# Regrouping the neighbourhood-attention stage of a two-layer diffusion backbone: pairs of heads as one step, other PSUM banks, another order of the filling work

## The chip, the cores and the metric

The kernel runs on one NeuronCore of a Trainium2 chip. Its inputs and outputs lie in HBM, everything is one launch. The metric is device time in microseconds (us), the median of several executions. The engines are named as in the profile: PE (TensorE, matrix multiplications and transposes), PEld (PE's weight loads), DVE (VectorE), ACT (ScalarE), POOL (GpSimd) and SP (SyncE, which here only issues DMAs).

## The reference

A backbone of two layers over 256 latent tokens and 256 context tokens of width 1024. Each layer is a half-step SwiGLU, a mixer, and a second half-step SwiGLU, each followed by a LayerNorm with residual. The mixer of layer 0, which this case is about, is neighbourhood attention with 16 heads of width 64: each latent query reads a 2-D window of the latent keys, with a bias for the relative position, and all context keys in the same softmax.

```python
qkv = (hx @ w_qkv).reshape(B, S, 3, N_HEADS, HEAD_DIM)
q = apply_axial_rope(qkv[:, :, 0], rope)
k = apply_axial_rope(qkv[:, :, 1], rope)
...
s_win = jnp.where(mask, s_win + bias.astype(jnp.float32)[None], -jnp.inf)
s_ctx = jnp.einsum('bjqhd,bchd->bhjqc', q_r, k_c).astype(jnp.float32) * scale
p = jax.nn.softmax(jnp.concatenate([s_win, s_ctx], axis=-1), axis=-1).astype(v.dtype)
return (jnp.einsum('bhjqk,bjkhd->bjqhd', p[..., :nk], v_blk)
        + jnp.einsum('bhjqc,bchd->bjqhd', p[..., nk:], v_c))
...
y_lat = jnp.moveaxis(o, 0, 1).reshape(B, S, D) @ w_out
```

The values are float32. The kernel keeps that accuracy by splitting each operand into a high and a low part: a product is three matmuls, high by high, high by low, low by high.

## The kernel before, in words

**Order.** PE's instructions run in the order in which the program writes them. The other engines' instructions are put in order by a scheduler at build time: by priority, which is the place in the program, moved forward by `tc.high_priority(offset=...)`, and by when it thinks that their inputs are there. At run time each engine works through its list in order.

**Units.** A unit is one step of a generator: six matmuls 128x512 (`mmu`, lines 152 to 159), for two chunks of 128 rows of the contraction. `wunit` (L162 to L182) loads the weights for units and splits them, ACT making the high part (L178), DVE the low part (L181). `tick` (L136) counts units. A `Late` (L113) is work that is written into the program so many ticks after it was made, or when somebody calls `get()`.

**PSUM.** There are eight banks in three groups: three "mm", three "at", two "tp". Panels and attention outputs use "mm" (`mmb`, L98), the scores S and the odd row tiles of the output projections use "at", transposes use "tp" (`tpb`).

**The attention stage** (L734 to L933). `q_half` projects and rotates q for eight heads (8 units), `kv_quarter` k and v for four heads (16 units). Each leaves a `Late`, which transposes the result (kT: L771 to L776, qT: L787 to L795) and splits it; `q_half` has a delay of two ticks, `kv_quarter` of one. For a pair of heads and one of two query tiles, `scores` (L804) makes S for both heads in two "at" banks with six matmuls; then per head DVE adds the bias (L818) and takes the maximum (L820), ACT takes the exponential (L822) and scales (L824). `probs_T` (L830) transposes one head's probabilities (L836) and splits them. `values` (L841) multiplies one head's with v into a "mm" bank, and adds the high and the low half of the product (L854, L855); after the second head of a pair the sum is split into oT (L861).

The loop (L902 to L930) runs over half steps, one head of one query tile each. In every second one it writes `scores` for a pair, in each one `probs_T` of the half step two before, and `values` one half step after a head's second `probs_T`. Between them `fill_some` writes units of the fill: first `filler` (k/v quarters 1 and 2, q half 1, k/v quarter 3: 56 units), with a rate of 2.4, 2.9 and 1.9 units per half step, and from half step 24 `last_filler`, which is the output projection (`sub_end`, `out_gemm` with `order_late`, 16 units, of which nine are given out in the loop at a rate of 1.0, and seven come after it).

**The output projection's order** (`order_late`, L421). A unit is (row tile t, column half n, contraction chunk u), with u from 0 to 3; chunk 3 needs the last four heads. Nine units of the three banks (0,0), (0,1), (1,0) with u up to 2 come first, then their u = 3, then all four units of bank (1,1). When row tile 0 is complete its LayerNorm runs, and five ticks later its transposes (hT, L340), on which the next stage begins.

Of the kernel before, what the change touches and what calls it, by code (L numbers as in the profile page):

```python
# [16 lines left out]
P = 128  # L17
# [18 lines left out]
LEAD = 5  # L36
TAIL = 3
XAT = 1
A_LAG = 2
A_PRE = 2  # L40
NX_AT = 2
R0 = 2.4
R1 = 2.9
R2 = 1.9
R3 = 1.0
LN_LAG = (5, 5)
LT_LAG = (5, 5)
F0_LAG = (5, 5, 6, 7)
G_LAG = 4
ROPE_EARLY = 70  # L50
S_EARLY = 40
V_LAG = 1
AHEAD = 3
P_EARLY = 70
V_EARLY = 70
W_HI = 2
# [8 lines left out]
def backbone_kernel(  # L65
# [22 lines left out]
    def nm(s):  # L88
        uid[0] += 1
        return f"{s}_{uid[0]}"  # L90

    def act(dt=F32, s="a"):
        return ap.tile([P, 512], dt, tag="act", name=nm(s))
# [4 lines left out]
    def mmb(s="mm", t=0):  # L98
        return bank("at" if t % 2 else "mm", s)

    def tpb(s="tp"):
        return bank("tp", s)

    def split(src, hi, lo):
        nc.scalar.activation(hi, src, AF.Copy)  # L105
        nc.vector.tensor_tensor(out=lo, in0=src, in1=hi.bitcast(F32), op=ALU.subtract)  # L106
# [311 lines left out]

        return order_skew(nu)[:-TAIL] + [(1, 1, u, c, c + 256) for c in (0, 256) for u in range(nu - TAIL, nu)]

    def order_late(nu):  # L421

        e = nu - 1
        banks = ((0, 0), (0, 1), (1, 0))
        o = [(t, n, u) for t, n in banks for u in range(e - 1)]
        o += [(t, n, u) for u in (e - 1, e) for t, n in banks]
        return o + [(1, 1, u) for u in range(nu)]

    def out_gemm(w, lhs, nk, order, evac, s, wrow0=0):

# [206 lines left out]
    def sub_end(w, lhs, nk, l, i, gm, wgt, nxt, s, order):  # L637


        gate = mod_rows(l, gm, "gate")  # L640
        lnr = None if nxt else ln_rows(l, i)
        GB = fold_cols(nxt[0], 0, nxt[1], (l, i)) if nxt else None
        st, hTs = {}, [None, None]

        def evac(t, n, bank, *c):
            if n == 0:
                st[t] = stat_tile(2 if nxt or t == 0 else 3)
            part = nxt is None and t == n == 1
            cs = slice(*(c or (0, 512)))
            residual(bank, xt[t][n][:, cs], gate[n][:, cs], wgt, None if c else ALPHA,  # L650
                     None if part and not c else st[t][:, n + (c[0] // 256 if c else 0)])
            if n == 1 and (not part or c and c[1] == 512):
                mv, rs = finish_stats(st[t])
                if nxt:
                    hTs[t] = modulated(xt[t], mv, rs, GB, (LN_LAG if nk > KC else LT_LAG)[t])
                else:
                    for h in range(2):
                        nc.vector.scalar_tensor_tensor(out=xt[t][h], in0=xt[t][h], scalar=mv[:, 0:1], in1=lnr[0][h],
                                                       op0=ALU.subtract, op1=ALU.mult)
                    for h in range(2):  # L660
                        nc.vector.scalar_tensor_tensor(out=xt[t][h], in0=xt[t][h], scalar=rs, in1=lnr[1][h],
                                                       op0=ALU.mult, op1=ALU.add)
                        sync.dma_start(out[0, t * P:(t + 1) * P, h * 512:(h + 1) * 512], xt[t][h])

        return out_gemm(w, lhs, nk, order, evac, s), hTs, (lambda: new_x(l, i))
# [86 lines left out]
    def kv_quarter(g, res):  # L752
        krs, v = [], []

        def each(t, bk):
            if t < 2:
                krs.append(roped(bk[:, 0:256], t, 1, 4))
            else:
                r1 = rtile(256)
                nc.scalar.activation(r1, bk[:, 0:256], AF.Copy)  # L760
                krs.append(r1)
            v.append(act(F32R, "v"))
            z = v[t].rearrange("p (h s d) -> p h s d", h=4, s=2)
            split(bk[:, 256:512].rearrange("p (h d) -> p h d", h=4), z[:, :, 0], z[:, :, 1])

        yield from tile_panel(D + g * 256, 2 * D + g * 256, [hTs[t] for t in range(4)], "wkv", each)

        def rest():
            kT = []
            for j in range(2):  # L770
                ps = tpb("kT")  # L771
                for t in range(4):
                    nc.tensor.transpose(ps[:, t * P:(t + 1) * P], krs[t][:, j * P:(j + 1) * P], ident)
                hi, lo = act(F32R, "kTh"), act(F32R, "kTl")
                split(ps, hi, lo)
                kT.append((hi, lo))  # L776
            return kT

        res.append((Late(1, rest), v))

    def q_half(g, res):
        qrs = []
        yield from tile_panel(g * 512, g * 512 + 256, [hTs[0], hTs[1]], "wq", lambda t, bk: qrs.append(roped(bk, t, 0, 8)))

        def rest():
            qT = []
            for j in range(2):  # L787
                ps = tpb("qT")
                for i in range(2):
                    for t in range(2):  # L790
                        nc.tensor.transpose(ps[:, i * 256 + t * P:i * 256 + (t + 1) * P],
                                            qrs[t][:, (2 * j + i) * P:(2 * j + i + 1) * P], ident)
                hi, lo = act(F32R, "qTh"), act(F32R, "qTl")
                split(ps, hi, lo)
                qT.append((hi, lo))  # L795
            return qT

        res.append(Late(2, rest))
# [37 lines left out]
            nc.tensor.transpose(pt[:, k * P:(k + 1) * P], pr[:, k * P:(k + 1) * P], ident)  # L836
        split(pt.rearrange("p (k q) -> p k q", k=4), pth[:, :, qt * P:(qt + 1) * P], ptl[:, :, qt * P:(qt + 1) * P])

    osum = {}

    def values(h):  # L841

        pth, ptl = PT.pop(h)
        ps = mmb("o")[:, 0:256]
        s = slice(h % 4 * P, (h % 4 + 1) * P)
        v = KV[h // 4][1]
        for k in range(4):
            nc.tensor.matmul(ps, v[k][:, s], pth[:, k], start=k == 0, stop=False)
            nc.tensor.matmul(ps, v[k][:, s], ptl[:, k], start=False, stop=k == 3)
        if h % 2 == 0:  # L850
            osum[0] = sp.tile([P, 512], F32, tag="tmp", bufs=3, name=nm("osum"))[:, 0:256]
        p0 = h % 2 * 64
        t = osum[0][p0:p0 + 64]
        nc.scalar.activation(t, ps[64:128], AF.Copy)  # L854
        nc.vector.tensor_tensor(out=t, in0=ps[0:64], in1=t, op=ALU.add)  # L855
        if h % 2:
            if len(oT) <= h // 4:
                oT.append([hp.tile([P, 512], F32R, tag="oT", bufs=6, name=nm("oT")) if len(oT) < 3 else act(F32R, "oT")
                           for _ in range(2)])
            cs = slice((h // 2 % 2) * 256, (h // 2 % 2) * 256 + 256)  # L860
            split(osum[0], *(z[:, cs] for z in oT[h // 4]))  # L861

    phase.__exit__(None, None, None)
    ext[0] = 0
# [12 lines left out]
    def last_filler():  # L877
        with tc.issue_after(bias_dma[-1].ins):
            for t in range(2):
                for h in range(2):  # L880
                    xt[t][h] = act(F32, "x")
                    sync.dma_start(xt[t][h], xscr[t * P:(t + 1) * P, h * 512:(h + 1) * 512])
            gen, nh, lt = sub_end(na_w_out[0], lhs_T(oT), KC, 0, 1, 5, 1.0, (0, 6), "wo", order_late(KU))
        box.extend([nh, lt])
        yield from gen

    box = []
    fill = filler()
    rate = [R0] * 8 + [R1] * 8 + [R2] * 8 + [R3] * 12
    credit = 0.0  # L890
    steps = [(h + i, qt) for h in range(0, NH, 2) for qt in range(2) for i in range(2)]
    prs = {}
    LAG = A_LAG
    fin = None

    def fill_some(n):
# [2 lines left out]
                break  # L899

    fill_some(A_PRE)
    for i in range(len(steps) + LAG + V_LAG):  # L902
        if i == NX_AT:
            new_x(0, 0, s2t)
            for t in range(2):
                for h in range(2):
                    sync.dma_start(xscr[t * P:(t + 1) * P, h * 512:(h + 1) * 512], xt[t][h])
        while i + AHEAD < len(steps) and len(KV) <= steps[i + AHEAD][0] // 4:
            fill_some(1)
        if i < len(steps) and i % 2 == 0:  # L910
            with tc.high_priority(offset=S_EARLY):
                prs[i], prs[i + 1] = scores(*steps[i])
            if i % 2 == 0 and i + 2 < len(steps):
                bias_pair(*steps[i + 2])
        credit += rate[min(i, len(rate) - 1)]
        n = int(credit)
        credit -= n
        if i >= 24 and fin is None:
            run(fill)
            fin = last_filler()  # L920
            fill = islice(fin, 9)
        fill_some((n + 1) // 2)
        if 0 <= i - LAG < len(steps):
            with tc.high_priority(offset=P_EARLY):
                probs_T(*steps[i - LAG], prs.pop(i - LAG))
        fill_some(n // 2)
        j = i - LAG - V_LAG
        if j >= 0 and steps[j][1] == 1:
            with tc.high_priority(offset=V_EARLY):
                values(steps[j][0])  # L930
    run(fill)
    run(fin)
    phase.__exit__(None, None, None)  # L933
# [129 lines left out]
```

## Time and profile before

| | |
|---|---|
| median of 3 runs | 1284.12 us (1282.69 to 1287.56) |
| the profiled execution, its own time | 1289.17 us |
| its span in the trace | 1287.4 us |
| PE busy | 1257.7 us, 98% |
| DVE busy | 955.1 us, 74% |
| ACT busy | 591.2 us, 46% |
| mean granted clock of PE | 0.996 |

The profiled execution is one, and somewhat longer than the median; 1.8 us of its time lie outside of the span. The attention loop lies between about 440 and 589 us of the span, the projection after it ends at about 602 us. In the profile's lists, "idle" is the time in which an engine's instruction waited, and the name behind the arrow is what released it. Matmuls are pipelined, so that the durations of neighbouring ones overlap: the distance between two starts tells more than a duration.

### The profile page before, as it was taken

The numbers are of one execution on the slowest core, as the hardware profiler recorded it, in microseconds if no ns is written. First come the engines' busy times: TensorE is split into PE (matmuls) and PEld (weight loads), VectorE is DVE, ScalarE is ACT, GpSimd is POOL, SyncE is SP. The second block draws the span as 40 slices with busy tenths as digits, with TensorE's granted clock in tenths as the row PEclk, the third lists the DMA queues.
The fourth block names the chain that finished last, engine by engine and source line by source line (L and its number), as shares of the span: only waits on it lengthen the run. The fifth ranks groups of instructions, "written<-read, shape, count | busy, mean of one in ns | idle before, by whom it ended". The sixth has DMA issues, their size and how long they took to land.

```text
span 1287.4 us, 17193 instructions
## 1 busy us (share of the span) xinstructions
PE 1257.7 (98%) x5890; PEld 1007.0 (78%) x5890; DVE 955.1 (74%) x1683; ACT 591.2 (46%) x1148; POOL 42.0 (3%) x71
## 2 busy tenths in 40 slices
PE   7999999999999999988999999999999999999997
PEld 4787778788778877766887787887787877788886
DVE  3699877485658777788998787757778788855545
ACT  2432132413236456686555435654435645655431
POOL 0000000000001111110000000000000000000000
PEclk9999999999999999999999999999999999999999
DMA  9977569484622744464999887666887764666641
GB/s 284 299 231 243 181 193 297 131 297 146 198 78 76 215 91 92 90 147 149 305 331 328 295 294 262 215 215 225 289 287 241 215 211 147 210 217 185 231 155 51
DMA packets 202712, 268.59 MB, mean 209 GB/s; under 512 B 30026, under 2 KB 149298, under 8 KB 202624
## 3 DMA queue, kind: packets, MB, share of 16 engines
q1 hardware_dynamic: 202624, 267.49, 65.9%
q8 instruction: 46, 0.75, 0.2%
q14 instruction: 42, 0.34, 0.1%
HBM read 265.27 MB, written 2.17 MB: 208 GB/s over the span
## 4 chain that ended last, share of the span: by engine, by line
PE 78%; DVE 8%; DMA 8%; ACT 3%; issue 2%; SPq 1%; POOL 0%; DVEq 0%; ACTq 0%
PE w L156 13%; PE w L157 13%; PE w L159 13%; PE f L541 6%; PE f L542 6%; PE f L543 6%; DMA ar<-in_ada_w_dram 5%; DMA w1r<-in_ffn_w_in_dram 2%; PE wkv L156 2%; PE wkv L157 2%; PE wkv L159 2%; PE wc L156 2%; PE wc L157 2%; PE wc L159 2%; DVE w1l L181 2%
## 5 line engine op out<-in xcount | busy, mean ns | idle before, releaser
L178 ACT ACTIVATE w1h<-w1r 128x512 fp32r<-128x512 f32 x352 | 203.3, 626 | 185.0 <-PE w L159 75.4
L181 DVE TENSOR_TENSOR w1l<-w1r,w1h 128x512 fp32r<-128x512 f32 x352 | 227.6, 684 | 66.5 <-ACT w1h L178 64.3
L156 PE MATMUL w<-w1h,hTh 128*128 128x512 f32 x528 | 211.6, 401 | 3.8 <-ACT hTh L105 3.7
L247 DVE SCALAR_TENSOR_TENSOR acc<-ar,cst,acc 128x512 f32<-128x512 f32 x266 | 187.2, 745 | 34.8 <-DMA ar<-in_ada_w_dram 34.8
L157 PE MATMUL w<-w1l,hTh 128*128 128x512 f32 x528 | 207.7, 393 | 0.0
L156 PE MATMUL w<-w2h,gh 128*128 128x512 f32 (+1 forms) x446 | 175.4, 394 | 0.0
L157 PE MATMUL w<-w2l,gh 128*128 128x512 f32 (+1 forms) x446 | 173.7, 390 | 0.3 <-DVE w2l L181 0.3
L178 ACT ACTIVATE w2h<-w2r 128x512 fp32r<-128x512 f32 x176 | 101.5, 624 | 140.9 <-PE w L159 131.6
L159 PE MATMUL w<-w1h,hTl 128*128 128x512 f32 x528 | 163.9, 392 | 0.6 <-DVE hTl L106 0.6
L181 DVE TENSOR_TENSOR w2l<-w2r,w2h 128x512 fp32r<-128x512 f32 x176 | 114.0, 686 | 43.5 <-ACT w2h L178 42.3
L541 PE MATMUL f<-h0h,w1h 128*128 128x512 f32 x352 | 139.8, 397 | 0.4 <-ACT w1h L178 0.4
L542 PE MATMUL f<-h0h,w1l 128*128 128x512 f32 x352 | 138.4, 393 | 0.0
L543 PE MATMUL f<-h0l,w1h 128*128 128x512 f32 x352 | 138.3, 393 | 0.0
L159 PE MATMUL w<-w2h,gl 128*128 128x512 f32 (+1 forms) x446 | 136.3, 387 | 0.0
L156 PEld LDWEIGHTS w<-w1h,hTh 128*128 128x128 f32 x528 | 99.5, 188 | 28.2 <-ACT hTh L105 5.5
L159 PEld LDWEIGHTS w<-w1h,hTl 128*128 128x128 f32 x528 | 99.5, 189 | 24.1 <-DVE hTl L106 1.4
L157 PEld LDWEIGHTS w<-w1l,hTh 128*128 128x128 f32 x528 | 99.6, 189 | 20.4 <-DVE w1l L181 0.3
L156 PEld LDWEIGHTS w<-w2h,gh 128*128 128x128 f32 x446 | 83.7, 188 | 21.7 <-issue 1.7
L157 PEld LDWEIGHTS w<-w2l,gh 128*128 128x128 f32 x446 | 83.8, 188 | 18.6 <-DVE w2l L181 1.3
L159 PEld LDWEIGHTS w<-w2h,gl 128*128 128x128 f32 x446 | 83.3, 188 | 18.7
L541 PEld LDWEIGHTS f<-h0h,w1h 128*128 128x128 f32 x352 | 66.6, 189 | 18.4 <-issue 3.7
L543 PEld LDWEIGHTS f<-h0l,w1h 128*128 128x128 f32 x352 | 66.5, 189 | 14.7 <-DVE h0l L519 0.3
(178 smaller groups left out, 1702.5 us busy)
## 6 DMA issues: line engine op xcount, KB each, us to landing
w1r<-in_ffn_w_in_dram SPq DMA_DIRECT2D x352, 256.0 KB
ar<-in_ada_w_dram SPq DMA_DIRECT2D x128, 512.0 KB
w2r<-in_ffn_w_out_dram SPq DMA_DIRECT2D x88, 512.0 KB
ar<-in_ada_w_dram SPq DMA_DIRECT2D x32, 256.0 KB
wkvr<-in_na_w_qkv_dram SPq DMA_DIRECT2D x32, 256.0 KB
wcr<-in_sc_w_in_dram SPq DMA_DIRECT2D x32, 256.0 KB
wqr<-in_na_w_qkv_dram SPq DMA_DIRECT2D x8, 512.0 KB
bias<-in_na_rpb_dram SPq DMA_DIRECT2D x64, 64.0 KB
```

What stands on the lines that cost most here:

```text
L156: nc.tensor.matmul(ps, lh, rh, start=first and i == 0, stop=False)
L157: nc.tensor.matmul(ps, lh, rl, start=False, stop=False)
L159: nc.tensor.matmul(ps, ll, rh, start=False, stop=last and i == n - 1)
L178: nc.scalar.activation(hi[:, a:a + m // W_HI], raw[:, a:a + m // W_HI], AF.Copy)
L181: nc.vector.tensor_tensor(out=lo[:, a:b], in0=raw[:, a:b], in1=hi[:, a:b].bitcast(F32), op=ALU.subtract)
L247: nc.vector.scalar_tensor_tensor(out=a, in0=src, scalar=sc, in1=a, op0=ALU.mult, op1=ALU.add)
L541: nc.tensor.matmul(ps, lh, hT0[k][0], start=(k == 0), stop=False)
L542: nc.tensor.matmul(ps, ll, hT0[k][0], start=False, stop=False)
L543: nc.tensor.matmul(ps, lh, hT0[k][1], start=False, stop=(k == KC - 1))
```

## The change

The loop now runs over whole steps: 16 steps of a pair of heads and one query tile, and one more iteration. In each, `scores` for the pair, half of the step's units, `probs_T` for both heads of the step before, the other half of the units, and after every second step `values` for the pair. `values` takes both heads: their products lie side by side in one bank, one ACT copy (512 wide instead of 256) and two DVE additions follow. kT and qT are transposed into "at" banks, those of S, and no longer into "tp". The rates per whole step are 5.0 (four steps), 4.8 (four), 4.0 (three), 3, and then 2, 1, 2, 1, 2. The output projection begins in step 11, after the last k/v quarter, whose kT is written there by `settle`. `order_late(KU, 1)` writes the unit (1,1,0) ahead of the three units with u = 3.

```diff
-A_LAG = 2
-NX_AT = 2
-R0 = 2.4
-R1 = 2.9
-R2 = 1.9
-R3 = 1.0
+NX_AT = 1
+W_FROM = 11
+R0 = 5.0
+R1 = 4.8
+R2 = 4.0
+R3 = [2, 1, 2, 1, 2]
...
-    def order_late(nu):
+    def order_late(nu, ahead=0):
...
-        o += [(t, n, u) for u in (e - 1, e) for t, n in banks]
-        return o + [(1, 1, u) for u in range(nu)]
+        o += [(t, n, e - 1) for t, n in banks] + [(1, 1, u) for u in range(ahead)] + [(t, n, e) for t, n in banks]
+        return o + [(1, 1, u) for u in range(ahead, nu)]
...
-                ps = tpb("kT")
+                ps = bank("at", "kT")
...
-                ps = tpb("qT")
+                ps = bank("at", "qT")
...
     def values(h):
-        pth, ptl = PT.pop(h)
-        ps = mmb("o")[:, 0:256]
-        s = slice(h % 4 * P, (h % 4 + 1) * P)
+        bk = mmb("o")
         v = KV[h // 4][1]
-        for k in range(4):
-            nc.tensor.matmul(ps, v[k][:, s], pth[:, k], start=k == 0, stop=False)
-            nc.tensor.matmul(ps, v[k][:, s], ptl[:, k], start=False, stop=k == 3)
...
+        for i in range(2):
+            pth, ptl = PT.pop(h + i)
+            ps = bk[:, 256 * i:256 * i + 256]
+            s = slice((h % 4 + i) * P, (h % 4 + i + 1) * P)
+            for k in range(4):
+                nc.tensor.matmul(ps, v[k][:, s], pth[:, k], start=k == 0, stop=False)
+                nc.tensor.matmul(ps, v[k][:, s], ptl[:, k], start=False, stop=k == 3)
+        t = sp.tile([P, 512], F32, tag="tmp", bufs=3, name=nm("osum"))
+        nc.scalar.activation(t[0:64], bk[64:128], AF.Copy)
+        for i in range(2):
+            nc.vector.tensor_tensor(out=t[64 * i:64 * i + 64, 0:256], in0=bk[0:64, 256 * i:256 * i + 256],
+                                    in1=t[0:64, 256 * i:256 * i + 256], op=ALU.add)
...
-            gen, nh, lt = sub_end(na_w_out[0], lhs_T(oT), KC, 0, 1, 5, 1.0, (0, 6), "wo", order_late(KU))
+            gen, nh, lt = sub_end(na_w_out[0], lhs_T(oT), KC, 0, 1, 5, 1.0, (0, 6), "wo", order_late(KU, 1))
...
+    steps = [(h, qt) for h in range(0, NH, 2) for qt in range(2)]
+    rate = [R0] * 4 + [R1] * 4 + [R2] * 3 + [3] + R3
...
+    for i in range(len(steps) + 1):
...
+        if i < len(steps):
             with tc.high_priority(offset=S_EARLY):
-                prs[i], prs[i + 1] = scores(*steps[i])
-            if i % 2 == 0 and i + 2 < len(steps):
-                bias_pair(*steps[i + 2])
+                prs[i] = scores(*steps[i])
+            if i + 1 < len(steps):
+                bias_pair(*steps[i + 1])
+        credit += rate[i]
         n = int(credit)
         credit -= n
+        fill_some((n + 1) // 2)
+        while i + 1 < len(steps) and len(KV) <= steps[i + 1][0] // 4:
+            fill_some(1)
+        if i:
+            h, qt = steps[i - 1]
+            with tc.high_priority(offset=P_EARLY):
+                for z, pr in enumerate(prs.pop(i - 1)):
+                    probs_T(h + z, qt, pr)
+        if i == W_FROM:
             run(fill)
+            settle()
             fin = last_filler()
             fill = islice(fin, 9)
         fill_some(n // 2)
+        if i and qt == 1:
             with tc.high_priority(offset=V_EARLY):
-                values(steps[j][0])
+                values(h)
```

More of the change, by code (lines that the diff above doesn't have):

```diff
@@ L51 @@
 S_EARLY = 40
-V_LAG = 1
-AHEAD = 3
 P_EARLY = 70
@@ L837, in probs_T @@
         split(pt.rearrange("p (k q) -> p k q", k=4), pth[:, :, qt * P:(qt + 1) * P], ptl[:, :, qt * P:(qt + 1) * P])
-    osum = {}
     def values(h):
-        pth, ptl = PT.pop(h)
-        ps = mmb("o")[:, 0:256]
-        s = slice(h % 4 * P, (h % 4 + 1) * P)
+        bk = mmb("o")
         v = KV[h // 4][1]
-        for k in range(4):
[L848 to L861, printed above, removed]
+        for i in range(2):
[10 more added lines that the diff above has]
+                                    in1=t[0:64, 256 * i:256 * i + 256], op=ALU.add)
+        if len(oT) <= h // 4:
+            oT.append([hp.tile([P, 512], F32R, tag="oT", bufs=6, name=nm("oT")) if len(oT) < 3 else act(F32R, "oT")
+                       for _ in range(2)])
+        cs = slice((h // 2 % 2) * 256, (h // 2 % 2) * 256 + 256)
+        split(t[:, 0:256], *(z[:, cs] for z in oT[h // 4]))
     phase.__exit__(None, None, None)
@@ L888, in backbone_kernel @@
     fill = filler()
-    rate = [R0] * 8 + [R1] * 8 + [R2] * 8 + [R3] * 12
+    steps = [(h, qt) for h in range(0, NH, 2) for qt in range(2)]
+    rate = [R0] * 4 + [R1] * 4 + [R2] * 3 + [3] + R3
     credit = 0.0
-    steps = [(h + i, qt) for h in range(0, NH, 2) for qt in range(2) for i in range(2)]
     prs = {}
-    LAG = A_LAG
     fin = None
@@ L901, in backbone_kernel @@
     fill_some(A_PRE)
-    for i in range(len(steps) + LAG + V_LAG):
+    for i in range(len(steps) + 1):
         if i == NX_AT:
@@ L907, in backbone_kernel @@
                     sync.dma_start(xscr[t * P:(t + 1) * P, h * 512:(h + 1) * 512], xt[t][h])
-        while i + AHEAD < len(steps) and len(KV) <= steps[i + AHEAD][0] // 4:
-            fill_some(1)
-        if i < len(steps) and i % 2 == 0:
+        if i < len(steps):
             with tc.high_priority(offset=S_EARLY):
-                prs[i], prs[i + 1] = scores(*steps[i])
-            if i % 2 == 0 and i + 2 < len(steps):
-                bias_pair(*steps[i + 2])
-        credit += rate[min(i, len(rate) - 1)]
+                prs[i] = scores(*steps[i])
+            if i + 1 < len(steps):
+                bias_pair(*steps[i + 1])
+        credit += rate[i]
         n = int(credit)
         credit -= n
-        if i >= 24 and fin is None:
+        fill_some((n + 1) // 2)
[7 more added lines that the diff above has]
+        if i == W_FROM:
             run(fill)
+            settle()
             fin = last_filler()
             fill = islice(fin, 9)
[L922 to L925, printed above, removed]
         fill_some(n // 2)
-        j = i - LAG - V_LAG
-        if j >= 0 and steps[j][1] == 1:
+        if i and qt == 1:
             with tc.high_priority(offset=V_EARLY):
-                values(steps[j][0])
+                values(h)
     run(fill)
```

## The prediction

> **What bounds the kernel now.** I read the page first, then the chain of waits, then PE's waits in the stretch that the change touches, then that stretch in windows.
>
> ```profile
> span 1287.4 us, 17193 instructions
> ## 1 busy us (share of the span) xinstructions
> PE 1257.7 (98%) x5890; PEld 1007.0 (78%) x5890; DVE 955.1 (74%) x1683; ACT 591.2 (46%) x1148; POOL 42.0 (3%) x71
> ```
> ```profile
> PE 78%; DVE 8%; DMA 8%; ACT 3%; issue 2%; SPq 1%; POOL 0%; DVEq 0%; ACTq 0%
> ```
>
> PE is the bound, and it carries 78% of the chain that ended last. The change adds and removes no matmul and no transpose, so it can only move the time in which PE stands still or runs slowly, and the page leaves 1287.4 - 1257.7 = 29.7 us of standing still in the whole kernel. This is what PE waited for from 438 to 604.5 us (engine, line, releaser: us in all, times, longest):
>
> ```profile
> PE kT L773 <- DVE pT L106: 2.0, 2, 1.5
> PE o L849 <- DVE pT L106: 1.5, 3, 0.6
> PE o L848 <- DVE osum L855: 0.9, 1, 0.9
> PE wo L156 <- ACT oT L105: 0.9, 1, 0.9
> PE o L848 <- ACT pT L105: 0.7, 1, 0.7
> PE w L159 <- DVE hTl L106: 0.6, 1, 0.6
> PE PT L836 <- DVE pT L106: 0.5, 1, 0.5
> PE w L156 <- ACT hTh L105: 0.3, 1, 0.3
> PE hT L340 <- DVE x L332: 0.3, 1, 0.3
> PE PT L836 <- DVE kTl L106: 0.2, 1, 0.2
> PE PT L836 <- DVE qTl L106: 0.2, 1, 0.2
> ```
>
> The rows on w and hT lie behind the loop. The other eight are the loop's and its projection's: 2.0 + 1.5 + 0.9 + 0.9 + 0.7 + 0.5 + 0.2 + 0.2 = 6.9 us in 11 waits. The windows (start and end, length, busy us of PE, PEld, DVE, ACT and POOL with instructions, granted clock, DMA share, GB/s) show where:
>
> ```profile
> 540.00:560.00 20.00, 16.74 (x97) 12.40 (x96) 17.43 (x38) 18.58 (x41) 3.52 (x4) 0.94 0.56 94
> 560.00:580.00 20.00, 19.50 (x114) 15.40 (x113) 15.67 (x35) 15.42 (x33) 4.94 (x6) 0.97 0.61 160
> 580.00:600.00 20.00, 16.87 (x89) 13.23 (x88) 15.25 (x33) 11.72 (x25) 1.61 (x3) 1.00 0.27 80
> ```
> ```profile
> 556.00:558.00 2.00, 1.45 (x8) 0.97 (x10) 2.00 (x6) 2.00 (x6) 0.74 (x1) 0.93 0.66 105
> 558.00:560.00 2.00, 2.00 (x7) 1.16 (x4) 2.00 (x5) 0.95 (x2) 0.00 (x0) 0.50 0.54 77
> 560.00:562.00 2.00, 2.00 (x10) 1.61 (x9) 1.44 (x3) 0.14 (x1) 1.83 (x2) 0.71 0.39 101
> ```
>
> From 540 to 560 us, when the 56 filling units have run out, PE stands 3.3 us, with ACT at 93% and DVE at 87%. From 580 to 600 us it stands 3.1 us. After the first of these the granted clock falls: (0.07 + 0.50 + 0.29) x 2 us = 1.7 us of work lost.
>
> A wait costs more than its idle time:
>
> ```profile
> 439.47 1.04 PE L773 MATMUL kT<-ident,kr 128*128 128x128 f32 x8
> 440.26 0.48 PE L156 MATMUL wkv<-wkvh,hTh 128*128 128x512 f32 x1
> 440.58 0.39 PE L157 MATMUL wkv<-wkvl,hTh 128*128 128x512 f32 x1
> 440.81 0.40 PE L156 MATMUL wkv<-wkvh,hTh 128*128 128x512 f32 x1
> ```
>
> A matmul takes 0.39 us, but the next starts after 0.23 us (440.58 to 440.81). Idle time counts from the end, so each pause costs 0.39 - 0.23 = 0.16 us more; 11 of them, 1.8 us. A unit is six starts, 1.4 us.
>
> **What goes.** In the new order no step of the loop runs out of units, both heads' products are in one bank, so that the second no longer waits for the first to be read (the row on osum), transposes of the probabilities no longer share banks with kT and qT, and the unit (1,1,0) lies between the last product and the units that need it. I let all eight rows go, with restarts and clock: 6.9 + 1.8 + 1.7 = 10.4 us. What is late in their place is below.
>
> **What costs nothing, I think.** Two heads' transposes together: eight take 0.79 us to the next start (439.47 to 440.26), two fours 0.36 us each,
>
> ```profile
> 452.21 0.60 PE L836 MATMUL PT<-ident,pr 128*128 128x128 f32 x4
> 452.57 0.47 PE L156 MATMUL wkv<-wkvh,hTh 128*128 128x512 f32 x1
> ```
>
> so 0.07 x 16 = 1.1 us lost at most, against 16 changes of instruction kind fewer; a change costs about 0.09 us (440.26 to 440.58 against 0.23), 1.4 us; I take 0. The wider ACT copy saves eight ACT instructions, off the path. new_x, with its DVE operations, row loads and stores, stays at step 1. The projection's loads on SP (weights, x, gate rows, columns) now come ahead of three bias pairs, each issued a step before its scores need it: 0, and if POOL's bias comes late it is in the tail's upper end.
>
> **What comes in.** The prices are from these rows (ns: min/median/max):
>
> ```profile
> L818 DVE TENSOR_TENSOR S<-S,bias x32: 410/423/433, 443.0 to 578.1; 128x256 f32<-128x256 f32 x32
> L820 DVE TENSOR_REDUCE mx<-S x32: 668/678/692, 443.6 to 579.1; 128x1 f32<-128x512 f32 x32
> L822 ACT ACTIVATE pr<-S,mx x32: 677/687/722, 444.4 to 580.8; 128x512 f32<-128x512 f32 x32
> ```
> ```profile
> L105 ACT ACTIVATE pT<-PT x32: 579/597/616, 453.1 to 585.7; 128x512 fp32r<-128x512 f32 x32
> L106 DVE TENSOR_TENSOR pT<-PT,pT x32: 673/690/693, 453.7 to 586.7; 128x512 fp32r<-128x512 f32 x32
> ```
>
> *Quarter 1's kT behind S.* Units are written 2 before the loop, then 5 a step: 17 by the end of step 2. The 17th closes quarter 1, one tick later its kT is due: right behind the scores of step 3. These hold two of the three "at" banks, the first kT takes the third, the second kT waits until a head's exponential has read its bank. That takes at least 0.42 + 0.68 + 0.69 = 1.8 us, and in the trace
>
> ```profile
> 506.24 0.40 PE L814 MATMUL S<-kTh,qTl 64*128 64x512 f32 x2
> ```
> ```profile
> 509.11 0.69 ACT L822 ACTIVATE pr<-S,mx 128x512 f32<-128x512 f32 x1 [0.21 <-DVE mx L820]
> ```
>
> 509.80 - 506.64 = 3.2 us. Less 0.4 us of the first four transposes: 1.4 to 2.8, I take 2.0. On PE everything is queued behind it. Quarter 2's kT (unit 34) has two units after step 6's scores, 2.8 us: 0.
>
> *qT in front of its scores.* By the end of step 7 there are 41 units; the 41st closes q half 1, and step 8's scores call its `get()` at once: qT has one unit of cover after its last projection, not the two ticks. In the trace, the last projection of q and the end of its rotation are
>
> ```profile
> 512.22 0.61 PE L159 MATMUL wq<-wqh,hTl 128*128 128x512 f32 x2
> ```
> ```profile
> 515.20 0.68 DVE L715 TENSOR_TENSOR qr<-qr,r 128x512 f32<-128x512 f32 x1
> ```
>
> 3.05 us apart; less the unit, 1.6, and less the two weight splits that DVE slipped in between, 0.3: I take 1.0. Then the second bank of S is that of the first qT: 0.60 + 0.69, less 0.4 of the second qT's transposes, 0.9 us and some 0.3 of hand-overs: 1.2. Together 2.2, from 1.2 to 4.0.
>
> *Quarter 0's kT* (one unit before the first scores, same bank): 1.8 us of cover against 1.3 and queues: 0.3, from 0 to 1.6.
>
> *The tail, steps 11 to 16*, with two units or one a step. The last transposes of probabilities come a unit, eight transposes and a unit after their scores, 3.6 us, 4.0 for the second head. That head's softmax needs 2 x 0.42 + 2 x 0.68 + 0.69 + some 0.7 for the scaling = 3.6, and ACT puts two high halves before it, 1.2: 0.8 us late. Step 12's scores wait for kT of quarter 3, written one unit earlier: 0.6. Step 14's second bank waits for an exponential of step 13: 0.3. Queues: 0.3. Sum 2.0, from 0.5 to the 3.3 + 3.1 = 6.4 that the same work loses now.
>
> *The unit put forward is missing later.* Now, row tile 0 is complete five units before the end, and its hT is written five ticks later, ahead of the last unit:
>
> ```profile
> 599.09 1.40 PE L340 MATMUL hT<-ident,x 128*128 128x128 f32 x8 [0.26 <-DVE x L332]
> ```
> ```profile
> 602.21 0.50 PE L156 MATMUL w<-w1h,hTh 128*128 128x512 f32 x1 [0.33 <-ACT hTh L105]
> ```
>
> Of the 602.21 - 600.49 = 1.7 us between these the last unit fills 1.4. With (1,1,0) put forward row tile 0 ends one unit later in the order, five ticks reach the end, and no unit is left behind hT: 1.4 us, from 0 (if DVE has less in front of hT) to 1.5.
>
> *Clock.* The new pauses are about 2 us each; one drop cost 1.7, and I put one at one in four: 0.4. [...]
>
> **Sum.** In: 2.0 + 2.2 + 0.3 + 2.0 + 1.4 + 0.4 = 8.3. Out: 10.4. The profiled execution of 1289.17 us (1.8 of it outside its span) would become 1287.1, and the median of 1284.12 us 1282.0, 0.2% less. About 0.5%, 6.4 us, is what a measurement of this kernel tells from no change.
>
> **Rivals.** *Faster.* DVE and ACT, no longer starved and flooded in turn, read the banks at the earliest: 1.4 + 1.2 + 0 + 0.5, and a weight buffer freed earlier by (1,1,0) lets DVE reach hT's low half sooner, so that this wait shrinks to nothing. In 3.1, out 10.4: 1276.8. For it speaks that 440 to 540 us hardly loses; against it, that the first three waits follow from the order whatever DVE does.
>
> *Slower: kT and qT hold S's banks until DVE comes to their low halves.* Off the scores' priority that is late:
>
> ```profile
> 467.03 1.04 PE L773 MATMUL kT<-ident,kr 128*128 128x128 f32 x8
> ```
> ```profile
> 470.23 1.27 DVE L106 TENSOR_TENSOR kTl<-kT,kTh 128x512 fp32r<-128x512 f32 x2
> ```
>
> The first low half ends 3.4 us after its transposes, behind weight splits. Then quarter 0 costs 3.4 - 1.8 = 1.6, quarter 3 too, q 1.0 + 3.4 - 0.4 = 4.0, quarter 1 the full 2.8: 10.0, and three clock drops 5.1. With 1.4 for the rest of the tail and 1.4 for hT it is 17.9 in, 10.4 out: 1291.6. It decides from about 3 us on. For it speaks DVE's 87% in the tail; against it, that qT is written under the scores' priority. [...]
>
> *The tail isn't mended*: its pauses come from ACT and DVE, not from missing units. Then it keeps 6.4 instead of 2.0: 1286.4, within 0.5%.
>
> **Chances.** The forecast 0.41, the unmended tail 0.11, faster by over 0.5% 0.28, slower 0.20; within 0.5%: 0.52. The forecast's own range is 1278.5 to 1286; the range that reaches into both rivals is 1276 to 1292.
>
> **What would show it.** Right: in the waits, kT from ACT pr or DVE kTl at step 3 with about 2 us, qT from DVE qr and S from DVE qTl before step 8, no o from osum, hT's wait moved to w from ACT hTh with about 2 us. Wrong: PE without gaps there, or more than 4 us lost in the last five steps, or a granted clock near 0.5 in two places.

## The result and the profile after

The changed kernel takes 1293.79 us in the median of 13 runs (1287.65 to 1298.99), the kernel before 1285.76 us in 13 runs beside it (1282.69 to 1288.88). The ratio is 1.0059, with a 95% interval from 1.0047 to 1.0072: 8 us slower, where no measurable change was forecast.

The page of the kernel after (its head, PE's row, the chain by engine):

```profile
span 1290.4 us, 17192 instructions
## 1 busy us (share of the span) xinstructions
PE 1258.1 (97%) x5890; PEld 1009.7 (78%) x5890; DVE 953.4 (74%) x1683; ACT 589.9 (46%) x1140; POOL 42.5 (3%) x71
...
PE 86%; DVE 5%; DMA 4%; ACT 3%; issue 1%; SPq 0%; POOL 0%; DVEq 0%; ACTq 0%
```

PE has the same work, and more of the chain is PE's own. The profiled execution took 1292.18 us, only 3.0 more than the profiled one of before. Before's one lost time far behind the changed stage where after's one waited for nothing:

```profile
PE w L156 <- ACT hTh L105: 2.7, 1, 2.7
PE hT L340 <- DVE x L332: 0.4, 1, 0.4
```
```profile
800.00:804.00 4.00, 4.00 (x12) 3.13 (x11) 3.90 (x8) 3.51 (x8) 0.44 (x1) 0.57 0.10 34
```

These are before's waits from 780 to 820 us and one of its windows: 2.7 + 0.4 us of waits, two restarts, and 0.43 x 4 = 1.7 us of clock, 5.1 us together. With them set aside the two profiled executions lie 8.1 us apart, as the medians do. So the stage must be compared by itself. From the first kT's start to the start of the next stage's first matmul, called the first w from here on, it took 602.21 - 439.47 = 162.7 us before; now it begins at 438.96 and ends at 610.92: 172.0 us.

```profile
610.92 0.50 PE L154 MATMUL w<-w1h,hTh 128*128 128x512 f32 x1 [2.01 <-ACT hTh L103]
```

What PE waits for in the stage, from 395 to 660 us, after (us in all, times, longest; the lines have moved up by one or two):

```profile
PE kT L772 <- ACT pr L821: 3.5, 2, 3.2
PE w L154 <- ACT hTh L103: 2.0, 1, 2.0
PE PT L835 <- DVE pT L104: 1.4, 1, 1.4
PE PT L835 <- ACT pr L823: 1.3, 1, 1.3
PE qT L790 <- DVE qr L714: 1.2, 1, 1.2
PE S L813 <- DVE kTl L104: 0.9, 2, 0.7
PE wo L154 <- ACT pr L821: 0.8, 1, 0.8
PE hT L338 <- DVE x L330: 0.7, 1, 0.7
PE S L813 <- ACT kTh L103: 0.6, 1, 0.6
PE S L813 <- DVE qTl L104: 0.6, 1, 0.6
PE wo L154 <- ACT oT L103: 0.6, 1, 0.6
PE S L813 <- ACT pr L821: 0.5, 1, 0.5
PE S L813 <- ACT qTh L103: 0.3, 1, 0.3
```

No o waits any more, neither for osum nor for pT, and kT no longer waits for pT. In their place stand 14.4 us in 15 waits, against 8.1 us in 14 before (all rows of the prediction's list, those on w and hT too). The windows show where, and what the clock did:

```profile
460.00:480.00 20.00, 16.80 (x84) 13.70 (x83) 14.05 (x29) 13.23 (x28) 2.21 (x3) 0.91 0.56 119
...
540.00:560.00 20.00, 20.00 (x114) 16.30 (x113) 15.15 (x34) 14.11 (x33) 3.15 (x4) 1.00 0.43 60
560.00:580.00 20.00, 17.73 (x94) 13.22 (x93) 15.02 (x34) 14.78 (x32) 3.65 (x5) 0.93 0.75 186
580.00:600.00 20.00, 16.61 (x94) 13.11 (x93) 13.84 (x30) 13.44 (x26) 0.73 (x1) 0.98 0.28 86
```
```profile
476.00:478.00 2.00, 2.00 (x7) 1.52 (x6) 0.69 (x1) 1.49 (x3) 0.00 (x0) 0.50 0.64 71
...
578.00:580.00 2.00, 2.00 (x10) 1.70 (x9) 0.33 (x2) 1.05 (x5) 0.72 (x1) 0.50 0.82 231
...
612.00:614.00 2.00, 2.00 (x6) 1.59 (x5) 1.29 (x3) 0.88 (x2) 1.00 (x2) 0.50 0.59 184
```

The hole from 540 to 560 us is filled, as the change does it: PE is busy through all 20 us. But new pauses stand at 472, 524 and in the last steps, and the granted clock is at 0.50 in three places instead of one. With the windows beside each, the one at 478 us loses (0.26 + 0.50 + 0.09) x 2 = 1.7 us, and the two others 1.7 each as well (0.16 + 0.50 + 0.19 and 0.13 + 0.50 + 0.22): 5.1 us against 1.7.

The account of the stage: 14.4 - 8.1 = 6.3 us more waits, one more restart 0.2, two more drops 3.4: 9.9 us. The stage is 172.0 - 162.7 = 9.2 us longer up to the first w. Right behind that lie nearly all of after's third drop, 1.7 more, and before's wait for hTl with its restart, 0.6 + 0.2 less: 10.1. So nearly all of the stage's difference is named. It is 2.0 more than the 8.1 above: after's trace is that much shorter elsewhere, 0.5 of it ahead of the stage. Over all runs the mean granted clock was 0.9939 in the kernel after, and 0.9959 to 0.9971 in the kernel before (in groups of runs on different chips): 0.002 to 0.0032 of 1258 us is 2.5 to 4 us. That mean covers the whole kernel, but in size it agrees with the 3.4 us of the one trace.

### The profile page after: what moved, and what is told of

Its sections match the earlier page's. It is cut to its first block, busy times and chain, and to the rows that moved or that the text cites. A ratio compares the mean times of both kernels' runs of the same rounds, so it can differ in the third digit from the quotient of the medians.

```text
span 1290.4 us, 17192 instructions
## 1 busy us (share of the span) xinstructions
PE 1258.1 (97%) x5890; PEld 1009.7 (78%) x5890; DVE 953.4 (74%) x1683; ACT 589.9 (46%) x1140; POOL 42.5 (3%) x71
## 4 chain that ended last, share of the span: by engine, by line
PE 86%; DVE 5%; DMA 4%; ACT 3%; issue 1%; SPq 0%; POOL 0%; DVEq 0%; ACTq 0%
PE w L154 15%; PE w L155 15%; PE w L157 15%; PE f L540 6%; PE f L541 6%; PE f L542 6%; DMA w1r<-in_ffn_w_in_dram 3%; PE wkv L154 2%; PE wkv L155 2%; PE wkv L157 2%; PE wc L154 2%; PE wc L155 2%; PE wc L157 2%; DMA ar<-in_ada_w_dram 1%; PE S L813 1%
```

## The experiments

Two theories stood against each other. *Cover*: kT and qT are now written where fewer units than their softmax or rotation needs lie between them and the work that holds or makes their data; the banks only decide which wait it is. *Banks*: kT and qT sharing S's banks is the cost by itself. Beside these, the put-forward unit, the paired product and the hole at 540 us were tried alone, and the clock.

**kT and qT back in the "tp" banks** (a_tp: the kernel after, with):

```diff
-                ps = bank("at", "kT")
+                ps = tpb("kT")
...
-                ps = bank("at", "qT")
+                ps = tpb("qT")
```

> The changed kernel with kT and qT back in the two tp banks, nothing else. Theory 1 (bank waits and the clock drop behind them are the largest part of the loss): the wait of kT for ACT pr (3.5 us in 2 waits) goes, the first scores' wait for kTl (0.9) and the scores' wait for qTl (0.6) shrink, qT's wait for its rotation (1.2) stays; one clock drop of 1.7 us fewer; 5 to 7 us faster than the changed kernel, so 1 to 3 us slower than before. Rival (the tail and the put-forward unit are the loss): not over 3 us faster than the changed kernel, and transposes of the probabilities wait for the banks that kT holds.

Measured: 1290.47 us, ratio 1.0039 [1.0022, 1.0056]. Its waits in the stage that differ from after's:

```profile
PE PT L835 <- DVE kTl L104: 2.1, 2, 1.5
...
PE kT L772 <- DVE pT L104: 1.8, 2, 1.4
```

kT's wait for pr is gone, and the drop at 475 us with it; the scores' waits for kTl and kTh (0.9 and 0.6) are gone too. But PT now waits for the bank that kT holds, and kT for the one that pT holds, as the rival had it. q's wait for its rotation, the waits from step 14 on and hT's are after's to 0.1 us. The banks carry about a third of the loss, 2.5 us as a point estimate (the intervals overlap), and two thirds stay.

**The projection's old order** (a_noahead: the kernel after, with):

```diff
-... "wo", order_late(KU, 1))
+... "wo", order_late(KU))
```

> The changed kernel without the unit put forward. Theory (the unit is only moved from in front of hT to in front of oT): w's wait for hTh falls from 2.0 us to about 0.5, its clock drop of 1.7 us goes, the wait of wo for oT rises from 0.6 to about 2.0; 1.5 to 2 us faster than the changed kernel, all of it the clock. Rival (the unit helps as it was meant to): 1 us slower, with the drop in another place.

Measured: 1293.14 us, 1.0051 [1.0031, 1.0071], level with after.

```profile
PE wo L154 <- ACT oT L103: 1.6, 1, 1.6
...
PE w L157 <- DVE hTl L104: 0.9, 2, 0.6
...
PE w L154 <- ACT hTh L103: 0.3, 1, 0.3
```

The unit is worth 1.0 us in front of oT (0.6 to 1.6) and costs 1.7 us behind hT (2.0 to 0.3, with 0.9 of hTl appearing): it moves a pause. The trace has no drop behind hT any more, two in the stage instead of three, and yet the time did not fall by the 1.5 to 2 us expected; the interval, 2.6 us to either side, is too wide to tell.

**Two units more before the loop** (a_pre4: the kernel after, with):

```diff
-A_PRE = 2
+A_PRE = 4
```

> The changed kernel with four units ahead of the loop instead of two, banks as changed. Then quarter 1's kT comes five units after scores instead of right behind them, and q half 1 is complete three units before its scores. Theory 1a (it is the missing cover, not the banks as such): the waits of kT for ACT pr (3.5), qT for DVE qr (1.2) and S for qTh and qTl (0.9) go to under 0.5 in all, with the clock drop near 475 us; 6 to 8 us faster than the changed kernel, about level with before. Rival 1b (kT in S's banks waits wherever it is put): kT keeps 1.5 us or more, and at most 3 us are won.

Measured: 1292.68 us, 1.0053 [1.0035, 1.0071], a miss: no better. Between 460 and 480 us PE now waits for nothing, and q's waits are gone. But the shift of two units puts quarter 2's kT behind step 6's scores, which the first of these PE rows shows, and the waits of the stage follow:

```profile
500.05 0.66 PE L772 MATMUL kT<-ident,kr 128*128 128x128 f32 x4
```
```profile
PE kT L772 <- ACT pr L821: 5.0, 2, 3.3
```

The same 3.3 us, one quarter later, and 1.7 more at the last quarter. The clock's drop has moved along: it stands near 506 us now and lasts 6.8 us instead of 3.4, in part while PE still waits. It is the place that costs, not the quarter.

**The put-forward unit alone** (b_ahead: the kernel before, with after's order_late and `order_late(KU, 1)`):

> The kernel before with only the unit (1,1,0) put forward. Theory: the wait of wo for oT (0.9 us and its restart) goes, w's wait for hTh rises from 0.3 to about 1.8; within 1 us of before, or 1.7 us slower where a clock drop follows. Rival (the unit is worth its wait): 1 us faster.

Measured: 1285.17 us, 0.9991 [0.9976, 1.0005]. Level: oT's wait of 0.9 is gone, w's for hTh has grown from 0.3 to 2.2.

**Cover given back** (a_cover: the kernel after, with):

```diff
-R0 = 5.0
-R1 = 4.8
+R0 = 5.25
+R1 = 5.0
...
-        res.append((Late(1, rest), v))
+        res.append((Late(4, rest), v))
```

The kT of quarters 1 and 2 are written four units after their projection instead of one, in the middle of a step, and the higher rates complete q's second half earlier; the last quarter's kT is written by `settle` in step 11, as in after. The banks, the paired product, the whole steps and the order of the projection are after's.

> The changed kernel, with its banks and its projection order, but kT due four ticks after its quarter instead of one, and rates of 5.25 and 5.0 instead of 5.0 and 4.8, so that no kT comes right behind scores and q half 1 is complete three units before its scores. Theory 1a (missing cover): kT's wait for ACT pr (3.5 us) falls under 0.5, the waits of qT and S for q (2.1) under 0.5, and the clock's drop near 475 us goes (1.7): 6 to 7 us faster than the changed kernel, about level with before. Rival 1b (kT in S's banks waits wherever it is put): under 2 us.

Measured: 1287.32 us, 1.0000 [0.9989, 1.0012]: level with the kernel before. The PE rows of quarter 1's kT, and its window:

```profile
470.34 0.39 PE L813 MATMUL S<-kTh,qTl 64*128 64x512 f32 x2
...
475.76 1.04 PE L772 MATMUL kT<-ident,kr 128*128 128x128 f32 x8
```
```profile
460.00:480.00 20.00, 20.00 (x111) 16.86 (x110) 16.66 (x36) 14.26 (x31) 2.22 (x3) 1.00 0.56 119
```

The eight transposes stand 5.4 us behind the scores and run in one piece. In after they came 0.32 us behind them and broke in two:

```profile
470.53 0.39 PE L813 MATMUL S<-kTh,qTl 64*128 64x512 f32 x2
470.85 0.65 PE L772 MATMUL kT<-ident,kr 128*128 128x128 f32 x4
474.70 0.93 PE L772 MATMUL kT<-ident,kr 128*128 128x128 f32 x4 [3.20 <-ACT pr L821]
```

a_cover's stage takes 604.45 - 440.28 = 164.2 us up to its first w, 7.8 less than after's. Its waits add up to 11.6 us in 14 (2.8 less than after's, one restart less), and up to the first w it has no drop of the clock where after has two (3.4): 6.4 of the 7.8; its one drop stands right behind the first w, as after's third does. What it gains in waits lies ahead of the last quarter: 0.8 us there, against 6.2 in after. At the last quarter's kT (0.6 + 1.6) and in step 14 (1.1 + 0.3) it waits longer than after does (0.6 + 0.2), and the other waits from step 14 on are after's. The stage is 1.4 us longer than before's, within the interval. With the other parts of the change kept, giving cover back takes away the loss, to within about 1.5 us, and about half of what it takes away in the trace is clock. The mean clock of its runs, 0.9964 against after's 0.9939, says much the same: 3 us.

**Filling the first pause with needless work** (a_warm: the kernel after, with quarter 1's first four transposes made seven times over; the data are the same):

```diff
-                for t in range(4):
+                for t in list(range(4)) * (7 if g == 1 and j == 0 else 1):
```

> The changed kernel, with the first four transposes of quarter 1's kT done seven times over, into the same bank, so that PE has 24 transposes (24 x 0.11 = 2.6 us) of needless work in its longest pause of 3.2 us. Theory (the clock answers to PE's standing still, and each drop is a price of its own): the second kT starts at the same time within 0.2 us, the pause is down to about 0.6 us, and the half-rate stretch near 475 us is gone: 1.7 us faster than the changed kernel, with more work. Rival (the drop comes from something else in that stretch, or transposes don't keep the clock up): same time or slower, drop still there.

Measured: 1293.54 us, 1.0040 [1.0025, 1.0055] (the kernel before beside it: 1287.39). The pause falls from 3.2 to 0.6 us and the clock stays at 1.00 from 470 to 480 us, but it now falls behind q's pause, where after's trace had 1.00:

```profile
526.00:528.00 2.00, 2.00 (x7) 1.16 (x6) 1.82 (x5) 0.00 (x0) 0.00 (x0) 0.50 0.46 152
528.00:530.00 2.00, 2.00 (x6) 1.52 (x6) 2.00 (x5) 1.61 (x5) 0.00 (x0) 0.50 0.87 258
530.00:532.00 2.00, 2.00 (x6) 1.54 (x5) 0.28 (x2) 0.45 (x1) 0.00 (x0) 0.50 0.58 44
```

With a shorter one behind hT these add up to 5.1 us again, as in after: two stretches instead of three. Whether a drop after the first pause is worth 1.7 us is not settled by this: its interval overlaps after's.

**Cover for the last quarter in the half-step loop** (b_late: the kernel before, with fewer units per half step and the projection from half step 23, the last kT written at once there):

```diff
-R2 = 1.9
+R2 = 1.45
...
-AHEAD = 3
+AHEAD = 1
...
-        if i >= 24 and fin is None:
+        if i >= 23 and fin is None:
...
+            settle()
```

> The kernel before with its fill spread to the end: R2 1.45 for 1.9, AHEAD 1 for 3, and the projection begun one half step earlier, after its kT is written (settle). Theory (PE's pauses from 544 to 557 us in the kernel before come from units that ran out): the waits of kT for DVE pT (2.0) and o for pT there (1.7) go, with the clock's drop (1.7): 4 to 6 us faster than before. Rival (ACT and DVE are full there): under 1.5 us, with the waits in other places.

Measured: 1290.71 us, 1.0024 [1.0010, 1.0037], a miss. The pauses of 547 to 557 us are gone, and quarter 1's kT waits 2.0 us for pT, the last quarter's 1.1 us for its rotation, PT 2.1 for pT. Near 590 us the clock stays down longest of all runs here; with the windows beside these it loses (0.08 + 0.50 + 0.50 + 0.20) x 4 = 5.1 us, ten us at half rate:

```profile
588.00:592.00 4.00, 3.08 (x11) 2.21 (x10) 1.33 (x3) 0.76 (x2) 0.00 (x0) 0.50 0.42 131
592.00:596.00 4.00, 3.48 (x9) 2.78 (x9) 1.78 (x4) 0.42 (x1) 0.00 (x0) 0.50 0.00 0
```

**The banks alone** (b_at: the kernel before, with kT and qT in "at"; a_tp's edit, the other way):

> The kernel before with kT and qT in S's banks, nothing else of the change. Theory 1a (cover decides): quarter 1's and 2's kT come late enough after scores to cost nothing, qT comes right behind the scores of the pair before and waits about 2.5 us, quarter 3's kT about 3 instead of 2: 3 to 5 us slower than before with a clock drop. Rival 1b (they wait wherever they are put): waits at all four places, over 6 us slower.

Measured: 1291.15 us, 1.0019 [1.0005, 1.0033]: 2.4 us slower by the ratio, 3.8 by the medians (1287.39 beside it), where 3 to 5 were expected.

```profile
PE qT L791 <- ACT pr L822: 3.1, 1, 3.1
...
PE S L814 <- ACT pr L822: 1.3, 1, 1.3
...
PE kT L773 <- ACT pr L822: 0.3, 1, 0.3
```

In the half-step loop qT happens to stand right behind scores (its first transpose 0.32 us after them) and pays 3.1 us; kT stands elsewhere and pays 0.3 in all, though at the last quarter's place S waits 1.3 us for a bank, where kT waited 2.0 in before. Same banks, other places, other waits: the bank costs most where a transpose follows scores. The clock loses 6.8 us in this trace, against 1.7 in before's.

**The paired product alone** (b_pair: the kernel before, with after's `values`, called after the second head):

> The kernel before with both heads' products in one bank, written after the second head's transposes; nothing else. Theory: the second head's wait for osum (0.9) goes, oT comes about 1 us later at the end (wo's wait for oT 0.9 to about 1.9): within 1.5 us of before. Rival (the one bank helps by itself): 2 us faster.

Measured: 1288.56 us, 1.0024 [1.0012, 1.0035], a miss: about 3 us slower, where at most 1.5 was expected.

```profile
PE S L814 <- ACT pr L822: 2.6, 2, 1.5
```

The wait for osum is gone as meant; S waits for pr instead, and the last oT comes later (1.6 us for 0.9).

**Whole steps alone** (a_whole: the kernel after with both edits, "tp" banks and the old order of the projection):

> The changed loop alone: whole steps, one bank for both heads' products and the new rates, with kT and qT in the tp banks and no unit put forward. Theory: without cover it loses in the tp banks instead, as with kT and qT put back alone (kT and the transposes of probabilities wait 3.9 us for each other, q 1.8), with one clock drop fewer because w waits 0.3 instead of 2.0 us for hTh: 2 to 4 us slower than before. Rival (the bank move and the unit are all of the loss): level with before.

Measured: 1291.32 us, 1.0043 [1.0027, 1.0058], 5.5 us slower and more than expected. With the paired product, the whole-step loop and its rates carry most of the loss without the banks and without the put-forward unit: PT waits 2.1 us for kTl, kT 1.8 for pT, q 1.1 for its rotation, and the last steps are after's but for oT (1.6 us for 0.6).

**The hole at 540 us alone** (b_hole: the kernel before, with units of the projection spread into it):

```diff
-R3 = 1.0
+R3 = 0.7
...
-    rate = [R0] * 8 + [R1] * 8 + [R2] * 8 + [R3] * 12
+    rate = [R0] * 8 + [R1] * 8 + [R2] * 6 + [R3] * 14
...
-        if i >= 24 and fin is None:
+        if i >= 22 and fin is None:
...
+            settle()
```

> The kernel before with nine output-projection units written earlier: rates of 1.9 for six half steps and then 0.7 for fourteen, the projection started from half step 22 instead of 24, the last quarter's kT written there at once. Half-step loop, one head per bank, tp banks and the order of the projection are unchanged. Theory A (PE's pauses between 544 and 560 us are missing units, since the 56 units of the first filler are used up): those pauses (kT, o and PT from pT, some 3 us) and the clock drop at 557 us go, 2 to 4 us faster than before, ratio 0.997 to 0.998. Rival B (ACT and DVE are full there, cover only moves): the waits turn up in the last half steps and on oT, PE's waits of the stretch stay within 1.5 us of before's and the time is level, ratio 0.999 to 1.002. Rival C: the kT written at once stands right behind its last projection and costs 1.5 to 3 us more, ratio 1.002 or above.

Measured: 1286.27 us, 0.9996 [0.9982, 1.0011]. The drop at 557 us is gone, and the waits add up to 9.0 us where before's were 8.1. Three rows of them, and 60 us of windows in one:

```profile
PE PT L836 <- DVE pT L106: 1.8, 3, 1.1
PE o L848 <- DVE osum L855: 1.6, 1, 1.6
PE wo L156 <- ACT pr L822: 1.3, 1, 1.3
```
```profile
540.00:600.00 60.00, 52.35 (x299) 40.57 (x297) 49.46 (x105) 46.78 (x102) 10.36 (x13) 1.00 0.50 119
```

PE stands for 60 - 52.35 = 7.65 us; before's same window has 53.11 busy us, part of them at half the clock. The hole was not only missing units: with the units spread otherwise, as many microseconds are waited for ACT and DVE, as the rival had it.

**A version with all of it** (v_best: a_cover with fewer units in steps 8 to 10, the last quarter's kT under the scores' priority, and the old order of the projection):

```diff
-R2 = 4.0
+R2 = 3.34
...
-            settle()
+            with tc.high_priority(offset=S_EARLY):
+                settle()
...
-... "wo", order_late(KU, 1))
+... "wo", order_late(KU))
```

> A version: the kernel with kT due four ticks later and the rates 5.25 and 5.0, and beside that R2 3.34 for 4.0 (quarter 3's kT comes three units after scores, not one), settle under the scores' priority, and no unit put forward. If cover is all that the changed order lacks, kT's waits of 2.2 us behind scores in step 11 go, S waits under 0.7 us for kT, w's wait for hTh falls from 2.0 to 0.3 and wo's for oT rises from 0.6 to 1.6; the loop's tail keeps about 5 us of waits. 2 to 4 us faster than before. Rival: a clock drop falls elsewhere, level with before.

Measured: 1286.08 us, 1.0004 [0.9991, 1.0017]. Its profiled execution has no drop in the stage and a stage of 600.27 - 440.00 = 160.3 us, 2.4 shorter than before's; the time over all runs does not show it, so the 2 to 4 us expected were missed. Its last steps still wait as in after: 1.4 (PT for pT), 1.3 (PT for pr), 0.9 (wo for pr), 1.6 (wo for oT). No version here beats the kernel before by more than its interval.

## Why the prediction was wrong

The range ended at 1292, and the time is 1293.79. The mechanisms were right nearly everywhere; the sizes were not. A measured price is the row of the waits plus 0.16 us for each restart.

| term | forecast | measured |
|---|---|---|
| quarter 0's kT | 0.3 | 0.7 + 0.2 = 0.9 |
| quarter 1's kT behind S | 2.0 | 3.2 + 0.2 = 3.4 |
| quarter 2's kT | 0 | 0.3 + 0.2 = 0.5 |
| qT in front of its scores | 2.2 | 1.2 + 0.6 + 0.3 + 0.5 = 2.6 |
| the tail | 2.0 | 5.8 |
| wo for oT | 0 | 0.6 + 0.2 = 0.8 |
| missing unit behind hT | 1.4 | 2.7 - 1.2 = 1.5 |
| clock | 0.4 | 5.1 |
| in | 8.3 | 20.6 |

Out went what the forecast said by releaser, 10.4 us, so the measured terms give 10.2 us net for the traces' stage, beside 10.1 seen.

**What held.** The order of units was read rightly: quarter 1's kT stands right behind step 3's scores, qT one unit after its projection, quarter 0's kT one unit before the first scores. hT's pause moved to w from ACT hTh and is 0.1 us off. The waits of o are gone. What was to show the forecast wrong has come: over 4 us lost in the last steps, and a clock of 0.50 in three places.

**The clock: 0.4 against 5.1.** This step failed worst. It counted one drop at one in four for all new pauses, though the slower rival beside it priced three. The trace of before had one drop among 11 waits (14 with those on w and hT), and I carried over that share; after has three drops in 15 waits. The share is no constant: a_cover has one in 14, b_hole and v_best none in 14 and 12. The drops that follow bank waits went from one (before's, behind kT) to two (at 475 and 578 us); the third follows w's wait for hTh, which is no bank wait. No wait of after's stage is longer than 3.2 us; before's drop follows waits of at most 1.5 us, after's at 578 us waits of 0.5 and 0.8 us.

**Quarter 1's kT: 2.0 against 3.4, above its range.** The range's end was 3.2 less 0.4, from before's trace; its lower end, the shortest chain through DVE and ACT, drew the value down. These are DVE's and ACT's rows there in after:

```profile
472.03 0.74 DVE L817 TENSOR_TENSOR S<-S,bias 128x256 f32<-128x256 f32 x2
473.15 1.28 DVE L819 TENSOR_REDUCE mx<-S 128x1 f32<-128x512 f32 x2
473.87 0.69 ACT L821 ACTIVATE pr<-S,mx 128x512 f32<-128x512 f32 x1 [0.63 <-DVE mx L819]
```

The exponential that frees the bank ends at 474.56, 3.6 us after the last scores end. DVE comes to the scores 1.1 us after their end, because a weight split (from 470.67) and the pair's sums (0.84 us from 471.27) stand in front; then it adds the bias for both heads before it takes the first maximum, and the exponential waits for that. The shortest chain, which has one head's bias and no queue, does not occur. The paired product is not the only cause: a_pre4 waits 3.3 us with no sums there, DVE being busy through all four us from 500 to 504, and b_at 3.1 us in the half-step loop.

**The tail: 2.0 against 5.8.** Step 12's scores for kT 0.6 + 0.2 + 0.3 = 1.1 (forecast 0.6), step 14's second bank 0.5 + 0.2 (0.3), PT for pr 1.3 + 0.2 (0.8), and two waits that the forecast had not. The first:

```profile
588.56 0.66 PE L835 MATMUL PT<-ident,pr 128*128 128x128 f32 x4 [1.41 <-DVE pT L104]
```

Both heads' transposes now stand side by side and need both "tp" banks, and these rows show who holds one of them:

```profile
584.85 0.24 PE L295 MATMUL mcT<-ident,mrow 32*128 32x32 f32 x1
590.49 0.18 DVE L297 COPY gcol<-mcT 128x32 f32<-128x32 f32 x1
```

mcT, a small transpose for the next stage's columns, is read by DVE only after 5.6 us. So the second head must wait until DVE has split the first (587.81 to 588.50; the step before's two splits had started at 580.40 and 581.25). No run moved mcT alone. The other: the unit (1,0,0), the first in its bank, waits 0.8 us for an "at" bank of the scores. This was the rival of the unmended tail, priced at 6.4, and it was given 0.11. b_hole supports it from the other side: more units at the hole did not shorten the waits. **oT:** the unit put forward leaves 0.6 of a wait that would be 1.6 without it (a_noahead), where I let all of it go.

**The rivals.** The slower one ended at 1291.6, near the time, by another mechanism. It let kT hold the banks of S until DVE reached its low half: S waits only 0.9 + 0.6 us for kTl and qTl. It is the reverse that costs most, S holding the bank of kT. What it named as its condition, DVE reaching low halves after about 3 us, did come: at quarter 1 the first low half ends 475.03 - 471.50 = 3.5 us after its transposes. But there and at quarter 2 the next scores come later than that, and before the first scores and step 12 more lay in between than the 1.8 us it reckoned with. The faster one fell with the first three waits, all of which came.

**What the experiments add.** a_cover settles it for the whole: with cover given back and the rest kept, the loss is gone. What is left open is how much of the mean 8 us is clock: 3 or so by all runs' clocks, but no run removed drops without moving pauses as well.

## What to carry to other kernels

When transposes are to share PSUM banks with work that other engines read, place them by where the bank has been read, not by where it is written: 0.3 us behind the scores they waited 3.1 to 3.3 us in three kernels, 5.4 us behind them nothing. Count every user of a group of banks: a transpose as small as mcT held one of two for 5.6 us. A unit of filling work moved to one pause is missing at another, so a regrouped loop must be counted out again step by step, with each transpose's distance to the work before and behind it. And price new pauses of 0.5 to 3 us on a full PE with the clock from the start, at 1.7 us each for some of them: from none to three in the stages shown here, each with 10 to 15 waits.

## What the runs showed of the hardware

Each of the three drops in after's stage cost the same, 1.7 us, which is half of a stretch of 3.4 us at a clock of 0.50, whatever the pause in front of it (waits of 0.5 and 0.8 us at 578, 3.2 us at 475, 2.0 us at 612). a_warm and b_late show longer stretches, 6.8 us (in rows from 526 to 532 and their neighbours) and about 10 us. The pause alone does not decide: q's three waits (1.2, 0.3 and 0.6 us) leave the clock at 1.00 in after and are followed by 6.8 us at 0.50 in a_warm, and the waits of 0.5 and 0.8 us in front of after's drop at 578 us stand in a_cover, between 564 and 572 us, with a clock of 1.00. In the one run that filled a pause, a drop stood at another place instead. Why the same pause sometimes costs a drop and sometimes not, no run here shows.
